# Up-projection weights of the FFN pairs 32 bytes off in longer buffers, and the inverse row sums in the forget weights' buffer

## The chip, the cores and the metric

The kernel runs on one core of one Trainium2 chip. The metric is the time of one execution on the device, in microseconds (us), as the median of several runs. Five engines work side by side and meet through semaphores: TensorE (PE in the profile; its weight loads are listed as PEld), VectorE (DVE), ScalarE (ACT), GpSimd (POOL) and SyncE (SP), whose queue issues most of the DMAs. On-chip memory (SBUF) has 128 partitions; a tile's place is given below as a byte address within each partition, which is the same for all of them.

## The reference

Two layers, each of three sub-layers on x (512 x 1024, float32): an FFN, a mixer with three branches, and a second FFN. Every sub-layer normalises x, shifts and scales it by values computed from c, and adds its gated result to x.

```
def swiglu(h, w_gate, w_up, w_down):
    return (jax.nn.silu(h @ w_gate) * (h @ w_up)) @ w_down

for l in range(2):
    mod = (silu(c) @ w_ada[l] + b_ada[l]).reshape(B, 9, 1024)
    h = modulate(rms_norm(x, norm_gain[l, 0]), mod[:, 0], mod[:, 1])
    x = x + 0.5 * mod[:, 2] * swiglu(h, w_gate[l, 0], w_up[l, 0], w_down[l, 0])   # 1024 -> 2816 -> 1024
    h = modulate(rms_norm(x, norm_gain[l, 1]), mod[:, 3], mod[:, 4])
    x = x + mod[:, 5] * hybrid_mixer(h, ...)
    h = modulate(rms_norm(x, norm_gain[l, 2]), mod[:, 6], mod[:, 7])
    x = x + 0.5 * mod[:, 8] * swiglu(h, w_gate[l, 1], w_up[l, 1], w_down[l, 1])
```

The mixer's branches are a chunked attention with a learned bias (a), a pooling branch (b) and a forgetting attention (c), whose per-head forget gates come from a small projection of h (1024 to 8). Both attentions divide by the row sums of their softmax.

## The kernel before

**Number format.** A product of float32 operands is made of three matmuls of a 32-bit matmul type: each operand is split into a high part (a cast by ScalarE) and a low part (a subtraction by VectorE), and `triple` (lines 117 to 122) issues high x high, high x low and low x high into the same accumulator. In the profile these are lines 119, 120 and 121. The first name behind the arrow is the moving operand, the second the stationary one (the weights, loaded by a PEld instruction of 128 x 128).

**FFN.** The 2816 hidden channels are 22 tiles of 128. They are worked in four parts of 6, 6, 4 and 6 tiles (`PARTS`). The first four or six tiles of the first part are worked one at a time (`plain`): 128 x 128 weights against all 512 tokens. All others are worked two at a time (`gate_up_pair`, `pair`): the 2 x 2 block product of two weight tiles, two halves of the 1024 channels and two halves of the tokens is done in seven block products in place of eight, as in Strassen's scheme. Each of the seven is 4 x 3 matmuls with 256 moving columns, so a pair of gate tiles and a pair of up tiles are 84 matmuls each. The order of the seven is that of the `prod` calls: a11, a12, s1, s2, a22, s4, s3. From the second part on, the up tiles are worked so too (`whole`); that is 8 up pairs in each of the four FFNs, 32 in all.

**Where the pairs' weights lie.** `pair_weights` makes the seven weight operands out of two loaded tiles. For gate tiles (`which` 0), a11, a12, s1 and a22 lie in `ptb` buffers (high and low part in one buffer), s2 and s4 in two `v2` buffers, s3 in two `strip` buffers. For up tiles (`which` 1), six of the seven lie in the three `whi` buffers (high parts) and the three `wlo` buffers (low parts), and s3 lies in one `v2` buffer. The same `whi` and `wlo` buffers hold the split weights of every other product of the program (`wchunk`): plain FFN tiles, the down projection, and all of the mixer. The moving operands of a pair are `hhi` and `hlo` (the split input) and block sums of it in `b` buffers; the high part of the sum for s3 lies in `pta`.

**Addresses.** A tag (the third argument of `st`) names a group of equal buffers; the groups lie one after another in the order of their first use, each buffer rounded up to 32 bytes. In the built program before the change, `hhi`, `hlo`, `b`, `xv`, `whi`, `wlo`, `ssum`, `t1` and `v2` begin at multiples of 128 bytes. Behind them follow small tiles of the normalisation, and `raw`, `pta`, `ptb`, `strip` and `t2` begin 32 bytes past a multiple of 128. Every step within these tiles that a pair uses is a multiple of 512 bytes.

**Order of the work.** A Python-side scheduler (`later`, `poll`) places small jobs between matmuls by a running count of PE work. Each engine then executes its own list in order; so does the SP queue with its DMAs: a DMA that waits for a buffer holds back all DMAs behind it. A DMA stands in the SP list at a place that depends on when its buffer comes free.

**Forget weights and row sums.** `forget` loads the 128 x 64 forget weights into the one `wf` buffer (256 bytes per partition), once in each layer (line 956). In each attention, `send` (line 1084) is called four times, for two heads each: it transposes the inverse row sums into PSUM, ScalarE copies them into the one `flat` buffer (512 bytes per partition on 8 partitions, line 1090), and POOL's queue writes them to memory (line 1092), from where `spread` reads them back to 64 partitions (line 1098).

Of the kernel before, what the change touches and what calls it, by code (L numbers as in the profile page):

```python
# [15 lines left out]
F32 = mybir.dt.float32  # L16
F32R = mybir.dt.float32r
# [5 lines left out]
P = 128  # L23
T = 512
D = 1024
# [6 lines left out]
NT = T // P  # L32
# [8 lines left out]
def encoder_kernel(tc, xT, c, w_ada, b_ada, gains, w_gate, w_up, w_down, w_qkv, w_f, w_ubg,  # L41
# [18 lines left out]
    def nm(s):  # L60
        uid[0] += 1
        return f"{s}_{uid[0]}"

    def st(shape, dt, tag, bufs):
        return sb.tile(shape, dt, tag=tag, bufs=bufs, name=nm(tag))

    def acc(shape=(P, T)):
        return ps.tile(list(shape), F32, tag="acc", bufs=4, name=nm("acc"))

    def mmt(shape=(P, T)):  # L70
        return ps.tile(list(shape), F32, tag="mm", bufs=4, name=nm("mm"))
# [26 lines left out]
    def later(delay, fn, group=None):  # L98
        t = Task(pe[0] + delay, fn, group)
        tasks.append(t)  # L100
        return t
# [77 lines left out]
    @contextlib.contextmanager  # L179
    def after(what):  # L180

        if what in last:
            with tc.issue_after(last[what]):
                yield
        else:
            yield
# [192 lines left out]
    def split_to(hi, lo, src, lo_eng=nc.vector):  # L379
        nc.scalar.copy(hi, src)  # L380
        return lo_eng.tensor_tensor(lo, src, hi.bitcast(F32), op=ALU.subtract).ins  # L381
# [61 lines left out]
    PARTS = (6, 6, 4, 6)  # L443
    UP_FROM = 1
    SPIN = (4, 0, 7, 3)


    class Ffn:
# [78 lines left out]
        def pair_weights(self, n, which=0):  # L527

            shape = [P, 2, 4, P]
            d = []  # L530
            if which:
                d = [(st(shape, F32R, "whi", 3), st(shape, F32R, "wlo", 3)) for _ in range(3)]
                both = st(shape, F32R, "v2", 4)
                e = (both[:, 0], both[:, 1])
            else:
                for _ in range(2):
                    both = st([P, 2] + shape[1:], F32R, "ptb", 2)
                    d.append((both[:, 0], both[:, 1]))
                d.append((st(shape, F32R, "v2", 4), st(shape, F32R, "v2", 4)))
                e = (st([P, 4, P], F32R, "strip", 2), st([P, 4, P], F32R, "strip", 2))  # L540
            r = [st(shape, F32, *(("raw", NRAW) if which else ("b", NB))) for _ in range(2)]
            for i in range(2):
                last["dma"] = nc.sync.dma_start(r[i].rearrange("p a k c -> p (a k) c"),
                                                (w_gate, w_up)[which][self.l, self.s, n + i]).ins
            s3 = st([P, 4, P], F32, "ssum", 1)
            a11, a12, a21, a22 = r[0][:, 0], r[0][:, 1], r[1][:, 0], r[1][:, 1]
            g = nc.vector.tensor_tensor

            def sums():
                split_to(*d[0], r[0])  # L550
                g(s3, a11, a21, op=ALU.subtract)
                g(a21, a21, a22, op=ALU.add)

            def more():
                g(a11, a21, a11, op=ALU.subtract)
                g(a12, a12, a11, op=ALU.subtract)
                split_to(*d[2], r[0])

            steps = [sums, lambda: split_to(*d[1], r[1]), more, lambda: split_to(*e, s3)]
            w = lambda i, j: (d[i][0][:, j], d[i][1][:, j])  # L560
            tiles = {"a11": w(0, 0), "a12": w(0, 1), "s1": w(1, 0), "a22": w(1, 1), "s2": w(2, 0), "s4": w(2, 1), "s3": e}
            return tiles, steps
# [170 lines left out]
        def start(self):  # L733
# [3 lines left out]
            def spin(operands, n):  # L737
                for z in range(n):
                    mm(acc((P, P)), ones, operands[z % len(operands)][:, :P], start=True, stop=True)
# [4 lines left out]
            for half in range(2):  # L744
# [3 lines left out]
                for tile_ in four[2:]:  # L748
                    fold = nc.vector.tensor_tensor(ssum, ssum, tile_, op=ALU.add)
                spin(four, SPIN[half])  # L750
                for t in range(NT):
                    last["sum"] = mm(pv[:, t:t + 1], ssum[:, t * P:(t + 1) * P], ones[:, 0:1], start=False,
                                     stop=half == 1, skip_group_check=True).ins
            spin([ssum], SPIN[2])
            gate["vector"] = fold.ins
# [14 lines left out]
            with after("turn"):  # L770
                spin([dg[:, 3, :]], SPIN[3])
            pgs = [(acc(), acc()), (acc(), acc()), (mmt(), mmt())]
# [232 lines left out]
    def attention(qs, ks, vs, strip, ys, filler, budget, group):  # L1005
# [5 lines left out]
        def logits(h, group_, strips):  # L1011
            p, odd = divmod(h, 2)
            (q, ql), k = qs[p], ks[p]
            s, lg, pr = mmt(), t1(T), t2(T)
            at = 0
            for i in group_:
                n = (i + 1) * P
                for z in (q, ql):
                    mm(s[:, at:at + n], z[:, odd, i * P:(i + 1) * P], k[:, odd, :n], start=z is q, stop=z is ql)
                at += n  # L1020
            at = 0
            for i in group_:
                n = (i + 1) * P
                mx = st([P, 1], F32, "mx", 4)
                nc.vector.tensor_tensor_reduce(out=lg[:, at:at + n], in0=s[:, at:at + n], in1=strips[i], scale=-1.0,
                                               scalar=BIG, op0=ALU.add, op1=ALU.min, accum_out=mx)
                if odd == 0 and i == 0:
                    sums[p] = st([P, 2 * NT], F32, "sm", 2)
                nc.scalar.activation(pr[:, at:at + n], lg[:, at:at + n], AF.Exp, bias=mx, scale=-1.0,
                                     accum_out=sums[p][:, odd * NT + i:odd * NT + i + 1])  # L1030
                pe[0] += 0.5 * (i + 1.5)
                at += n
            if odd and i == NT - 1:
                later(LAG_S, lambda: send(p), group)
            later(LAG_T, lambda: turn(h, group_, pr), group)
# [48 lines left out]
        def send(p):  # L1084
            rs = st([P, 2 * NT], F32, "rs", 1)
            nc.vector.reciprocal(rs, sums[p])
            tp = mmt()
            nc.tensor.transpose(tp[:2 * NT, :P], rs, ident)
            flat = st([2 * NT, P], F32, "flat", 1)
            nc.scalar.copy(flat, tp[:2 * NT, :P])  # L1090
            pe[0] += 0.5
            nc.gpsimd.dma_start(inv_dram[group, p], flat)
            later(LAG_R, lambda: spread(p), group)

        def spread(p):
            for off in range(2):
                r = inv_dram[group, p].rearrange("(h i) q -> h (i q)", h=2)[off:off + 1, :]
                nc.gpsimd.dma_start(rows_of[p][off * HD:(off + 1) * HD, 1, :], r.broadcast_to([HD, T]))
            later(LAG_N, lambda: norm_rows(p), group)
# [293 lines left out]
```

## Time and profile before

| what | value |
|---|---|
| median of 3 runs | 2378.53 us (2377.65 to 2382.12) |
| the profiled execution's own time | 2377.12 us |
| its span, first to last instruction | 2375.4 us |
| TensorE busy, matmuls | 2356.8 us (99%), 14172 |
| VectorE busy | 1781.4 us (75%) |
| ScalarE busy | 1168.7 us (49%) |
| GpSimd busy | 190.6 us (8%) |
| granted TensorE clock | 1.000 of full speed |

The page of the profile gives the busy time of each engine, the span in 40 slices, the chain of work that ended last, and the costliest groups of instructions. A matmul's duration in it is the time from its start to its modelled end, and the next one starts before that; so the pace of a stream of matmuls is read from the difference of their starts in the timeline, in which a row is: start in us, duration in us, engine, line, operation, tiles (out<-in), shapes and count. A remark in square brackets at a row's end is idle time before it; a row without one followed without a gap.

### The profile page before, as it was taken

The page shows a single profiled execution, that of the slowest core. Times are in us where ns is not written, and L with a number is a line of the kernel's source. Part 1 is how long each engine was busy: PE and PEld are TensorE (multiplying, and loading weights), DVE is VectorE, ACT ScalarE, POOL GpSimd, SP SyncE. Part 2 cuts the span into 40 slices and gives each one's busy share as a digit, 9 for nine tenths or more (in the row PEclk, how much of TensorE's full clock was granted, in tenths as well). Part 3 has the DMA queues.
Part 4 walks back from the last instruction along what each step waited for, and adds up shares of the span by engine and source line. Part 5 has one row for each costly group of instructions (what it writes and reads, how often), then busy time and mean ns, then how long its engine had stood idle before and what let it go on. Part 6 is the DMA issues. An engine that isn't in the chain of part 4 may idle for free. (4 is left out here: it accounts for less than half of the span.)

```text
span 2375.4 us, 36727 instructions
## 1 busy us (share of the span) xinstructions
PE 2356.8 (99%) x14172; PEld 2092.4 (88%) x14172; DVE 1781.4 (75%) x3213; ACT 1168.7 (49%) x2048; POOL 190.6 (8%) x309
## 2 busy tenths in 40 slices
PE   8999999999999999999999999999999999999999
PEld 6898998788888898999998999988888888989998
DVE  7888876787678477888678778776866774767784
ACT  5354455676532353544554444556765324544452
POOL 2000002122220000000100000120222101000000
PEclk9999999999999999999999999999999999999999
DMA  7634433333367425344325333423243763223232
GB/s 278 207 104 155 148 125 99 95 98 120 123 211 265 154 68 187 111 137 150 109 87 188 128 104 134 160 89 99 87 136 114 260 233 133 89 98 123 64 116 89
DMA packets 118484, 325.19 MB, mean 137 GB/s; under 512 B 12034, under 2 KB 14338, under 8 KB 118308
## 3 DMA queue, kind: packets, MB, share of 16 engines
q1 hardware_dynamic: 115106, 314.38, 39.5%
q0 software_dynamic: 3200, 8.46, 1.1%
q8 instruction: 111, 1.82, 0.3%
q14 instruction: 65, 0.53, 0.1%
q10 hardware_dynamic: 2, 0.00, 0.0%
HBM read 316.35 MB, written 6.44 MB: 136 GB/s over the span
## 5 line engine op out<-in xcount | busy, mean ns | idle before, releaser
L272 ACT CAST whi<-raw 128x1024 fp32r<-128x1024 f32 (+1 forms) x260 | 270.4, 1044 | 345.5 <-PE acc L120 196.2
L274 DVE TENSOR_TENSOR wlo<-raw,whi 128x1024 fp32r<-128x1024 f32 (+1 forms) x254 | 310.1, 1225 | 155.1 <-ACT whi L272 153.2
L120 PE MATMUL acc<-b,whi 128*128 128x512 f32 (+1 forms) x704 | 261.1, 371 | 2.0 <-DVE b L381 2.0
L119 PE MATMUL acc<-b,whi 128*128 128x512 f32 (+1 forms) x704 | 262.3, 373 | 0.0
L121 PE MATMUL acc<-b,wlo 128*128 128x512 f32 (+1 forms) x704 | 260.4, 370 | 1.2 <-DVE wlo L274 1.2
L121 PE MATMUL mm<-b,wlo 128*128 128x256 f32 (+1 forms) x768 | 244.8, 319 | 0.3 <-DVE wlo L274 0.3
L120 PE MATMUL mm<-b,whi 128*128 128x256 f32 (+1 forms) x768 | 244.5, 318 | 0.0
L119 PE MATMUL mm<-b,whi 128*128 128x256 f32 (+1 forms) x768 | 244.5, 318 | 0.0
L198 DVE CUSTOM_DVE_ANT_0 v<-v,b,badac 128x1024 f32<-128x1024 f32 x144 | 187.2, 1310 | 19.6 <-DMA v<-in_w_ada_dram 19.5
L120 PE MATMUL mm<-hlo,whi 128*128 128x256 f32 (+1 forms) x616 | 199.1, 323 | 0.0
L121 PE MATMUL mm<-hhi,wlo 128*128 128x256 f32 (+1 forms) x616 | 199.0, 323 | 0.0
L119 PE MATMUL mm<-hhi,whi 128*128 128x256 f32 (+1 forms) x616 | 198.7, 323 | 0.0
L120 PE MATMUL acc<-hlo,whi 128*128 128x512 f32 x480 | 188.1, 392 | 1.7 <-DVE hlo L788 1.6
L119 PE MATMUL acc<-hhi,whi 128*128 128x512 f32 x480 | 187.9, 396 | 1.1 <-ACT hhi L785 1.1
L121 PE MATMUL acc<-hhi,wlo 128*128 128x512 f32 x480 | 187.6, 391 | 0.0
L380 ACT CAST whi<-raw 128x1024 fp32r<-128x1024 f32 x96 | 100.8, 1050 | 136.0 <-PE mm L120 68.0
L121 PEld LDWEIGHTS mm<-b,wlo 128*128 128x128 f32 x768 | 146.3, 190 | 11.2 <-DVE wlo L274 1.2
L120 PEld LDWEIGHTS mm<-b,whi 128*128 128x128 f32 x768 | 146.3, 191 | 10.2
L119 PEld LDWEIGHTS mm<-b,whi 128*128 128x128 f32 x768 | 146.3, 191 | 10.1
L120 PEld LDWEIGHTS acc<-b,whi 128*128 128x128 f32 x704 | 132.7, 189 | 25.2 <-DVE b L381 3.8
L121 PEld LDWEIGHTS acc<-b,wlo 128*128 128x128 f32 x704 | 132.6, 188 | 24.2 <-DVE wlo L274 1.7
L119 PEld LDWEIGHTS acc<-b,whi 128*128 128x128 f32 x704 | 132.7, 189 | 21.6
(326 smaller groups left out, 6116.9 us busy)
## 6 DMA issues: line engine op xcount, KB each, us to landing
v<-in_w_ada_dram SPq DMA_DIRECT2D x144, 512.0 KB, 4.8
raw<-in_w_down_dram SPq DMA_DIRECT2D x88, 512.0 KB, 3.9
raw<-in_w_up_dram SPq DMA_DIRECT2D x82, 512.0 KB, 3.6
b<-in_w_gate_dram SPq DMA_DIRECT2D x76, 512.0 KB, 6.0
raw<-in_w_ubg_dram SPq DMA_DIRECT2D x56, 512.0 KB, 4.1
raw<-in_w_qkv_dram SPq DMA_DIRECT2D x42, 512.0 KB, 4.0
raw<-in_w_branch_dram SPq DMA_DIRECT2D x24, 512.0 KB, 3.6
raw<-in_w_out_dram SPq DMA_DIRECT2D x16, 512.0 KB, 3.7
```

Source lines behind the costliest of these rows:

```text
L119: mm(o, lh, rh, start=start, stop=False, skip_group_check=onto)
L120: mm(o, lh, rl, start=False, stop=False, skip_group_check=onto)
L121: mm(o, ll, rh, start=False, stop=stop, skip_group_check=onto)
L198: dot = nc.vector.tensor_tensor_reduce(out=raw, in0=raw, in1=silc[0], scale=1.0, scalar=badac[:, l, j, d:d + 1], op0=ALU.mult, op1=ALU.add ...
L272: nc.scalar.copy(hi, raw)
L274: last["lo"] = lo_eng.tensor_tensor(lo, raw, hi.bitcast(F32), op=ALU.subtract).ins
L380: nc.scalar.copy(hi, src)
```

## The change

Two edits. In `pair_weights`, the six up-pair operands in `whi` and `wlo` are views that begin 8 elements (32 bytes) into a buffer of 1024 + 16 elements, so that the group's buffers are 4160 bytes long in place of 4096. `wchunk` still takes its tiles from the start of the same buffers. In `send`, the tile of the inverse row sums takes its buffer from the group `wf`, which grows from 256 to 512 bytes; the group `flat` is gone.

```
     PARTS = (6, 6, 4, 6)
     UP_FROM = 1
     SPIN = (4, 0, 7, 3)
+    SHIFT = 8
...
             shape = [P, 2, 4, P]
             d = []
             if which:
-                d = [(st(shape, F32R, "whi", 3), st(shape, F32R, "wlo", 3)) for _ in range(3)]
+                d = [tuple(st([P, D + 2 * SHIFT], F32R, t, 3)[:, SHIFT:SHIFT + D].rearrange("p (a k c) -> p a k c", a=2, k=4)
+                           for t in ("whi", "wlo")) for _ in range(3)]
                 both = st(shape, F32R, "v2", 4)
                 e = (both[:, 0], both[:, 1])
...
             nc.vector.reciprocal(rs, sums[p])
             tp = mmt()
             nc.tensor.transpose(tp[:2 * NT, :P], rs, ident)
-            flat = st([2 * NT, P], F32, "flat", 1)
+            flat = st([2 * NT, P], F32, "wf", 1)
             nc.scalar.copy(flat, tp[:2 * NT, :P])
```

What the built program makes of it, as bytes past a multiple of 128:

| tiles | before | after |
|---|---|---|
| `hhi`, `hlo`, `b`, `xv`, `ssum`, `t1`, `v2` | 0 | 0 |
| `whi`, the three buffers, used from their start | 0, 0, 0 | 0, 64, 0 |
| `wlo`, the three buffers, used from their start | 0, 0, 0 | 64, 0, 64 |
| up pairs' six operands in `whi` / `wlo` | 0 / 0 | 32, 96, 32 / 96, 32, 96 |
| `raw`, `pta`, `ptb`, `strip`, `t2` | 32 | 32 |

In numbers of matmuls: 2304 with 256 columns (32 pairs x 72) get weights 32 bytes past a multiple of 64. Without such a shift, weights 64 bytes past a multiple of 128 are met by 2160 matmuls with 512 columns and 400 with 256, and a moving operand there by 448 with 512.

The order of the instructions on PE, DVE, ACT and POOL is the same. On the SP queue one DMA moves: the load of layer 1's forget weights, whose buffer is now also that of the row sums. These are the rows of the SP queue in layer 0 around its place before, at the mixer's first projections (`raw` are the loads of projection weights):

```order
L261 DMA raw_3628<-in_w_down_dram 128x2x512
L261 DMA raw_4008<-in_w_qkv_dram 128x2x512
L261 DMA raw_4086<-in_w_qkv_dram 128x2x512
L956 DMA wf_16368<-in_w_f_dram 128x64
L261 DMA raw_4116<-in_w_qkv_dram 128x2x512
L261 DMA raw_4146<-in_w_qkv_dram 128x2x512
```

In the changed kernel the rows there follow each other without it:

```order
L261 DMA raw_3628<-in_w_down_dram 128x2x512
L261 DMA raw_4008<-in_w_qkv_dram 128x2x512
L261 DMA raw_4086<-in_w_qkv_dram 128x2x512
L261 DMA raw_4116<-in_w_qkv_dram 128x2x512
L261 DMA raw_4146<-in_w_qkv_dram 128x2x512
```

The DMA now stands later in layer 0, behind the last branch load of the forgetting attention's stretch and ahead of the load of the pooling weights (`t`) and of silu(c) (`b`). The SP queue there in the changed kernel:

```order
L261 DMA raw_6999<-in_w_ubg_dram 128x1024
L261 DMA raw_7060<-in_w_branch_dram 128x2x512
L958 DMA wf_16368<-in_w_f_dram 128x64
L1168 DMA t_1300_6850<-in_w_pool_dram 128x4x128
L1287 DMA b_6848<-sil_dram 128x1024
L261 DMA raw_7066<-in_w_ubg_dram 128x1024
```

Before, `t` followed the branch load at once. What the moved DMA waits for there is the release of its buffer by the last row sums of layer 0, that is, by POOL's write of them to memory. The numbers behind the tiles' names only tell buffers apart.

More of the change, by code (lines that the diff above doesn't have):

```diff
@@ L445, in encoder_kernel @@
     SPIN = (4, 0, 7, 3)
+    SHIFT = 8
     class Ffn:
@@ L531, in pair_weights @@
             if which:
-                d = [(st(shape, F32R, "whi", 3), st(shape, F32R, "wlo", 3)) for _ in range(3)]
+                d = [tuple(st([P, D + 2 * SHIFT], F32R, t, 3)[:, SHIFT:SHIFT + D].rearrange("p (a k c) -> p a k c", a=2, k=4)
+                           for t in ("whi", "wlo")) for _ in range(3)]
                 both = st(shape, F32R, "v2", 4)
@@ L1088, in send @@
             nc.tensor.transpose(tp[:2 * NT, :P], rs, ident)
-            flat = st([2 * NT, P], F32, "flat", 1)
+            flat = st([2 * NT, P], F32, "wf", 1)
             nc.scalar.copy(flat, tp[:2 * NT, :P])
```

## The prediction

> **What bounds the kernel now.** I read the page first, then the windows over the stretches in which up pairs run, then the timeline of TensorE there.
>
> ```profile
> span 2375.4 us, 36727 instructions
> PE 2356.8 (99%) x14172; PEld 2092.4 (88%) x14172; DVE 1781.4 (75%) x3213; ACT 1168.7 (49%) x2048; POOL 190.6 (8%) x309
> ```
>
> TensorE is busy 99% of the span. What shortens its stream of matmuls shortens the kernel; what only moves other engines does nothing until TensorE waits. Next, a stretch of three gate pairs and three up pairs in the second FFN of layer 0, and ten us of it:
>
> ```profile
> core 0: us, PE busy (x) PEld busy (x) DVE busy (x) ACT busy (x) POOL busy (x), PEclk, DMA share, GB/s
> 947.68:1007.75 60.07, 60.07 (x506) 60.07 (x504) 48.74 (x86) 32.10 (x58) 0.00 (x0) 1.00 0.32 99
> 977.70:987.70 10.00, 10.00 (x86) 10.00 (x85) 9.90 (x18) 6.62 (x12) 0.00 (x0) 1.00 0.01 2
> ```
>
> TensorE never waits, at the full granted clock (1.00): 504 matmuls (two more are cut by the window's edges) in 60.07 us, 119.2 ns each. VectorE is at 81%, though at 99% in the second row. The pace inside one pair, by the starts of the matmuls:
>
> ```profile
> 947.68 0.28 PE L119 MATMUL acc<-hhi,ptb 128*128 128x256 f32 x1
> ...
> 951.94 0.28 PE L119 MATMUL acc<-b,v 128*128 128x256 f32 x1
> ...
> 953.37 0.28 PE L119 MATMUL acc<-b,ptb 128*128 128x256 f32 x1
> ...
> 954.79 0.28 PE L119 MATMUL acc<-hhi,v 128*128 128x256 f32 x1
> ...
> 956.23 0.28 PE L119 MATMUL acc<-pta,strip 128*128 128x256 f32 x1
> ...
> 957.65 0.28 PE L119 MATMUL mm<-hhi,whi 128*128 128x256 f32 x1
> ...
> 966.16 0.28 PE L121 MATMUL mm<-hhi,wlo 128*128 128x256 f32 x1
> ```
>
> All are the same matmul, 128 x 128 weights and 256 columns. The gate pair's products with weights in `ptb` (36, then 12) take 4.26 + 1.42 = 5.68 us: 118.3 ns each. The two with weights in `v2` take 1.43 and 1.44 us for 12: 119.2 and 120.0. The one in `strip` takes 1.42: 118.3. The up pair, weights in `whi` and `wlo`, takes 8.51 us for 71 steps: 119.9 each. `ptb` and `strip` lie 32 bytes past a multiple of 64, `v2`, `whi` and `wlo` on one. So the place of the weights costs or saves 1.6 ns of a matmul with 256 columns.
>
> **The shifted weights.** 32 up pairs have 72 matmuls each in `whi` and `wlo`, 2304 in all. Their price changes from 119.9 to 118.3 ns: 2304 x 1.6 ns = 3.7 us, or 0.12 us in each pair. The starts are rounded to 0.01 us, which leaves about 0.3 ns on the difference of the two paces and so 0.7 us on the sum. All of it lies on the path, since TensorE has no gap here. The seventh product (s3, weights in `v2`) stays on its multiple of 64.
>
> What no row shows is high and low parts that alternate between 32 and 96 past a multiple of 128, as the shifted ones do: in `ptb` and `strip` both are at 32. Bounds: 0 us if one operand at 96 brings the even pace back, 4.4 us (3.7 + 0.7) if all run like `ptb`. I take 3.7, because the two paces seen so far go with the place past a multiple of 64, and 96 is 32 past one.
>
> A page speaks against this. The Trainium skill (SBUF — State Buffer, section on the DMA port swizzle) gives SBUF lines of 16 bytes, with a price for crossing to a new line; 32 bytes are two whole lines, so by it the shift alters nothing and the sum would be 0. The rows at 951.94 and 953.37 disagree: weights in `v2` and in `ptb`, two products of one pair, take 1.43 and 1.42 us, and the longer runs go at 119.9 and 118.3 ns.
>
> **Engines that write the shifted tiles.** ScalarE casts and VectorE subtracts into them:
>
> ```profile
> L381 DVE TENSOR_TENSOR wlo<-raw,whi 128x1024 fp32r<-128x1024 f32 x96 | 117.2, 1220 | 23.3 <-ACT whi L380 23.2
> L381 DVE TENSOR_TENSOR ptb<-b,ptb 128x1024 fp32r<-128x1024 f32 x70 | 85.6, 1222 | 32.0 <-ACT ptb L380 31.6
> ```
>
> Writing to `ptb`, 32 bytes off, costs VectorE 1222 ns against 1220 on the multiple: 2 ns in 96 instructions, 0.2 us and not on the path. ScalarE's casts precede these and have the same cover as below. A pair that is 0.12 us shorter leaves VectorE less room, so I looked for how early it is:
>
> ```profile
> 967.48 1.22 DVE L381 TENSOR_TENSOR wlo<-raw,whi 128x1024 fp32r<-128x1024 f32 x1
> 977.67 0.28 PE L119 MATMUL mm<-hhi,whi 128*128 128x256 f32 x1
> ```
>
> The last low part for the second up pair of the stretch is ready at 968.70, and that pair begins at 977.67: 9.0 us of cover against 0.12 lost. Without cover VectorE would set the pace at 48.74 of 60.07 us, which is still shorter. I take 0.
>
> **The plain tiles that come to lie 64 bytes on.** Half of the `whi` and `wlo` buffers now begin 64 bytes past a multiple of 128. No row has 128 columns of weights there. The nearest are the forget projection's weights (40 columns, 160 bytes apart, so at 0, 32, 64 and 96 in turn, each used twice), beside two rows of what a matmul with 512 columns can cost:
>
> ```profile
> 652.04 0.39 PE L121 MATMUL acc<-hhi,wlo 128*128 128x512 f32 x1
> ...
> 663.60 0.39 PE L121 MATMUL acc<-hhi,wlo 128*128 128x512 f32 x1
> ```
>
> ```profile
> 372.26 0.40 PE L119 MATMUL acc<-ptb,hhi 128*128 128x512 f32 x1
> ...
> 376.46 0.50 PE L338 MATMUL mm<-ones,strip 128*128 128x1 f32 x4
> ```
>
> ```profile
> 421.50 0.40 PE L963 MATMUL mm<-hhi,ssum 128*40 128x512 f32 x1
> 421.97 0.39 PE L963 MATMUL mm<-hhi,ssum 128*40 128x512 f32 x1
> 422.42 0.40 PE L963 MATMUL mm<-hhi,ssum 128*40 128x512 f32 x1
> 422.89 0.39 PE L119 MATMUL acc<-whi,hhi 128*128 128x512 f32 x1
> ```
>
> All on multiples of 128: 51 steps in 11.56 us, 226.7 ns. Moving operand 32 past (`ptb`): 18 in 4.20 us, 233.3 ns; so here being off is slower, by 6.7. The forget weights, two matmuls each: 0.47 us at 32, 0.45 at 64, 0.47 at 96. So 64 does not run like 32 and 96, and its 225 ns a matmul are nearest to the 226.7 on multiples of 128. I take 0 for the 2160 + 448 matmuls of 512 columns. The bounds: if 64 were like 32 by these rows (235 ns), 2608 x 8.3 = 21.6 us more; if it really gave 225 to the 2160, 3.7 us less, and with the 400 of 256 columns at 1.6 ns 0.6 more of that.
>
> **The moved load of the forget weights.** Before, it was issued as soon as its old contents were read, and blocked nothing:
>
> ```profile
> 377.32 0.34 SPq L956 DMA_DIRECT2D wf<-in_w_f_dram  x1
> 388.59 43.13 SPq L261 DMA_DIRECT2D raw<-in_w_qkv_dram  x9
> ```
>
> The next load came 11 us later, held by its own buffer; taking the DMA away gives 0. At its new place it waits for POOL's last write of the row sums:
>
> ```profile
> 647.21 0.51 POOL L1092 DMA_DIRECT2D inv_dram_c<-flat  x1 [8.65 <-ACT flat L1090]
> 649.56 1.08 POOL L1098 DMA_DIRECT2D b<-inv_dram_c  x2 [1.83 <-PE acc L121]
> ```
>
> ```profile
> 648.55 0.42 SPq L1166 DMA_DIRECT2D t<-in_w_pool_dram  x1
> 660.53 2.07 SPq L261 DMA_DIRECT2D raw<-in_w_ubg_dram  x2
> ```
>
> ```profile
> 652.79 0.62 ACT L380 CAST pta<-t 128x512 fp32r<-128x512 f32 x1 [2.02 <-DMA t<-in_w_pool_dram]
> 656.19 0.62 ACT L380 CAST b<-b 128x512 fp32r<-128x512 f32 x1 [2.78 <-DVE b L1105]
> ```
>
> The read-back at 649.56 follows that write's landing, so the forget load goes out at about 649.6 and the pooling weights at about 650.0, 1.4 us later than before, and silu(c) behind them likewise. Late next is ScalarE's cast of them, at 654.2 and done by 654.8; the instruction behind it began at 656.19 for another reason. The next projection load, at 660.53, is not reached. So 0 on the path, with 1.4 us as the price if it were not covered. The shared buffer adds no other wait that bites: the row sums come only behind the forget projection of their own layer, and layer 1's forget weights are not read before layer 1's mixer.
>
> **Sum.** The profiled execution took 2377.1 us, 1.7 more than its span; less 3.7 is 2373.4. The median of the runs shown is 1.4 above it, and I forecast on that scale: 2378.5 - 3.7 = 2374.8 us.
>
> **The rivals.** (1) The pace does not come with the address alone, or not at 96, and stays at 119.9. For it: gate and up pairs differ in PSUM banks, and `ptb` holds high and low part in one buffer. Against it: `strip` holds them in two and runs at 118.3. Time 2378.5. The 16-byte lines of the Trainium skill's SBUF page would give this result. (2) 64 past a multiple of 128 breaks the even step of the 512-column matmuls as 32 does. The place is every plain FFN tile, the down projection and the mixer; it ends above the old time as soon as a matmul there loses 1.4 ns (3.7 us / 2608), and at half the bound, 10.8 us, it gives 2385.6. For it: the 233.3 ns row. Against it: the forget weights at 64. (3) A wait takes the 0.12 us of each pair back, VectorE being at 99% for ten us. Against it: 9.0 us of cover. Time up to 2378.5. (4) The plain tiles at 64 gain too, by the other bound, 3.7 + 0.6: 2370.5. For it: the one 0.45 us step of the forget weights. Against it: two matmuls of 40 columns, rounded to 0.01 us, say little of 2160.
>
> **How the numbers follow.** Forecast 0.57, (1) 0.17, (2) 0.11, (3) 0.05, (4) 0.10. Above or below 0.2% (4.8 us) is about what a measurement of this kernel can tell from no change; the three runs shown differ by 4.5. The forecast's gain, 3.7, lies under that by 1.1, and with the runs' scatter I give it 0.4 to come out as faster, 0.57 and a little to stay within. Faster: 0.57 x 0.4 + 0.10 x 0.9 = 0.32. Slower: nearly all of (2) and a trace of the others, 0.13. Within: 0.55. The range 2371.0 to 2381.0 holds the forecast, (1) and (3) with the runs' scatter and about half of (4), and leaves (2) out.
>
> **What would show it.** In the changed profile the steps of the up pairs' 72 matmuls should go from 119.9 to a mean of 118.3 ns, and the six-pair stretch from 60.07 to 59.72 us with no idle time on TensorE. The 512-column steps should stay at 226.7. The forget load should be issued near 649.6 and the pooling weights' cast begin near 654.2 with TensorE untouched. A longer 512-column step would make the forecast wrong on the slow side, an unchanged 119.9 in the up pairs would make it no change.

## The result, and the profile after

The changed kernel takes 2392.8 us (median; 2390.6 to 2398.2) where the kernel before, run beside it, takes 2381.4 (2377.7 to 2383.5): a ratio of 1.0052, with a 95% interval of 1.0041 to 1.0062. It is slower by about 12 us, and the forecast was 2374.8. The profiled execution took 2393.4 us.

The comparisons of pace below are read as in the prediction: the difference of the starts of two matmuls, divided by the number of steps between them. First the page of the profile after the change:

```profile
span 2391.6 us, 36728 instructions
PE 2370.8 (99%) x14172; PEld 2090.1 (87%) x14172; DVE 1781.6 (74%) x3213; ACT 1165.1 (49%) x2048; POOL 193.7 (8%) x309
```

The span has grown by 16.2 us and TensorE's busy time by 14.0, with the same 14172 matmuls; VectorE's busy time is what it was. So only 2.2 us of the growth is idle time of TensorE; for the rest, its matmuls follow each other more slowly. The timeline of TensorE after the change, for the products of 512 columns that ran at 226.7 ns before (the prediction's rows from 652.04 to 663.60):

```profile
651.71 0.40 PE L119 MATMUL acc<-hhi,whi 128*128 128x512 f32 x1
...
653.76 0.39 PE L119 MATMUL acc<-hhi,whi 128*128 128x512 f32 x1
...
654.45 0.40 PE L119 MATMUL acc<-hhi,whi 128*128 128x512 f32 x1
...
664.16 0.39 PE L119 MATMUL acc<-hhi,whi 128*128 128x512 f32 x1
```

From 651.71 to 653.76 are nine steps, 227.8 ns each; by the built program's addresses both weight tiles there begin on a multiple of 256 bytes. From 654.45 to 664.16 are 42 steps in 9.71 us, 231.2 ns each; there the high and low parts begin 128 and 64 past a multiple of 256, then 64 and 192. This is the same kind of work as in the prediction's rows, at a pace 4.5 ns slower. Next, the timeline of a gate pair and an up pair in the six-pair stretch:

```profile
951.83 0.28 PE L119 MATMUL acc<-hhi,ptb 128*128 128x256 f32 x1
...
956.14 0.28 PE L119 MATMUL acc<-b,v 128*128 128x256 f32 x1
...
961.83 0.29 PE L119 MATMUL mm<-hhi,whi 128*128 128x256 f32 x1
...
970.25 0.28 PE L121 MATMUL mm<-hhi,wlo 128*128 128x256 f32 x1
```

The up pair's 71 steps take 8.42 us, 118.6 ns in place of 119.9: the shift gains here, with four fifths of the forecast's size. But the gate pair's 36 steps with weights in `ptb` take 4.31 us, 119.7 ns in place of 118.3, though nothing in the diff touches them. The windows view of that stretch (columns as in the prediction):

```profile
951.83:1011.79 59.96, 59.96 (x505) 59.94 (x504) 47.84 (x83) 32.01 (x58) 0.00 (x0) 1.00 0.31 98
```

59.96 us in place of 60.07: 0.11 less, where 0.35 was forecast, again without a gap on TensorE and at the full granted clock.

Over the whole execution, the time from each matmul's start to the next one's, summed by the kind of weights in the two traces (worked out from all starts; what a step has above 400 ns at 512 columns, or above 200 at 256, is counted as waiting):

| steps | count | ns per step, before to after | change, us |
|---|---|---|---|
| weights in `whi`, `wlo`, 512 columns, into `acc` | 3168 | 230.0 to 233.4 | +10.7 |
| weights in `whi`, `wlo`, 512 columns, into `mm` | 1464 | 227.7 to 231.1 | +4.9 |
| `whi`, `wlo` moving, 512 columns | 1008 | 235.9 to 237.0 | +1.1 |
| `v2` and `ptb` moving, 512 columns | 216 | 226.7 to 232.6 (`v2`) | +0.7 |
| weights in `whi`, `wlo`, 256 columns, up pairs among them | 3071 | 120.1 to 118.7 (`mm`) | -4.7 |
| weights in `ptb`, 256 columns | 1968 | 118.2 to 119.6 (`acc`) | +2.8 |
| weights in `v2`, 256 columns | 1224 | 119.7 to 118.5 (`acc`) | -1.1 |
| waiting | | | +2.7 |
| all others | | | -1.2 |
| sum | | | +15.9 |

The 4632 matmuls of 512 columns with weights in `whi` and `wlo` carry +15.6 of the 15.9 us, but not all of it is pace. Near 1530 us TensorE waits 3.2 us for a low part from VectorE, and the seven steps behind that wait take about 427 ns each; the granted clock from 1532 to 1540 is 0.79. The trace before has no such steps. Five of the kernels below whose wide tiles all lie on multiples of 256 bytes have seven or eight of them at this point of the program, so they are no effect of the place. With the steps above 300 ns left out, the mean of the 4632 goes from 227.8 to 230.8 ns, which is +13.8 us. The named rows together, with this +13.8, make +12.6 us, and the ratio of 1.0052 is 12.4 us. The two profiled executions are further apart, by 16.2 us: they also differ in waiting and in that slow stretch, and the one before took 2377.1 us, less than its median of 2381.4.

By the place of the weights after the change (the next table), the 13.8 us are 8.6 from weights at 64 and 192, 3.2 from weights at 128, and 2.0 from weights that stayed at 0 between moved ones.

The table of places under "The change" counts past a multiple of 128. Past a multiple of 256, which turned out to matter, they are, before and after:

| tiles | before | after |
|---|---|---|
| `whi`, three buffers | 0, 0, 0 | 0, 64, 128 |
| `wlo`, three buffers | 0, 0, 0 | 192, 0, 64 |
| `ssum`, `t1`, `v2` | 0 | 128 |
| `raw`, `pta`, `ptb`, `strip`, `t2` | 32 | 160 |

The names from `raw` to `t2` are called the late group below. The moved DMA, in the SP queue and on ScalarE after the change:

```profile
649.96 0.33 SPq L958 DMA_DIRECT2D wf<-in_w_f_dram  x1
650.34 0.43 SPq L1168 DMA_DIRECT2D t<-in_w_pool_dram  x1
```

```profile
655.92 0.62 ACT L380 CAST pta<-t 128x512 fp32r<-128x512 f32 x1 [4.34 <-DMA t<-in_w_pool_dram]
```

The forget load goes out at 649.96 (forecast about 649.6) and the pooling weights' cast begins at 655.92 (forecast 654.2); TensorE is then in the run of 42 steps shown above, without a gap.

### The profile page after: what moved, and what is told of

Same layout as the page of the kernel before. It is cut to its first block, busy times and chain, and to the rows that moved or that the text cites. A ratio compares the mean times of both kernels' runs of the same rounds, so it can differ in the third digit from the quotient of the medians.

```text
span 2391.6 us, 36728 instructions
## 1 busy us (share of the span) xinstructions
PE 2370.8 (99%) x14172; PEld 2090.1 (87%) x14172; DVE 1781.6 (74%) x3213; ACT 1165.1 (49%) x2048; POOL 193.7 (8%) x309
```

## The experiments

Five theories were set against each other. **A**: the longer buffers take plain tiles off multiples of 256 bytes, and that breaks the even step at 512 columns. **B**: the 32-byte shift itself slows plain tiles. **C**: the shared buffer and the moved load cost. **D**: only the unequal places of high and low part count. **E**: 32 past a multiple of 64 is what quickens the up pairs. Unless something else is said, the kernel before is what is edited, and ratios are to it.

### The second edit alone

```diff
-            flat = st([2 * NT, P], F32, "flat", 1)
+            flat = st([2 * NT, P], F32, "wf", 1)
```

> The kernel before with the second edit alone: the inverse row sums in the forget weights' buffer, so the forget load moves in SP's list, and no address of whi, wlo, v2, raw, ptb or strip changes. Theory A (the longer buffers move the plain tiles off multiples of 256 bytes and break the even step of 512-column matmuls): within 0.1% of before, 512-column steps at 226 to 227 ns as before. Theory C (the shared buffer and the moved load cost the time): about 12 us slower.

Measured: 2380.2 us, ratio 1.0000 (0.9991 to 1.0009). The shared buffer and the moved DMA cost nothing that shows beyond 2 us either way, where theory C had about 12. Theory C falls.

### Longer buffers, no shift

```diff
-                d = [(st(shape, F32R, "whi", 3), st(shape, F32R, "wlo", 3)) for _ in range(3)]
+                d = [tuple(st([P, D + 16], F32R, t, 3)[:, 0:0 + D].rearrange("p (a k c) -> p a k c", a=2, k=4)
+                           for t in ("whi", "wlo")) for _ in range(3)]
...
-            flat = st([2 * NT, P], F32, "flat", 1)
+            flat = st([2 * NT, P], F32, "wf", 1)
```

> The changed kernel without the 32 bytes: buffers 4160 bytes long, up pairs' tiles at their start, so every tile of whi and wlo lies 0, 64, 128 and 192, 256, 320 past a multiple of 512. Theory A: the 512-column matmuls are as slow as in the changed kernel, about 16 us against before; up pairs now on multiples of 64 run at 114 to 117 ns instead of 118.6, which gives up to 8 us back, so 4 to 16 us slower than before. Theory B (the 32 bytes themselves slow the plain tiles that use the buffers afterwards): as before.

Measured: 2388.2 us, ratio 1.0032 (1.0021 to 1.0044). The timeline of the same 42 steps of 512 columns:

```profile
654.26 0.39 PE L119 MATMUL acc<-hhi,whi 128*128 128x512 f32 x1
...
663.96 0.39 PE L119 MATMUL acc<-hhi,whi 128*128 128x512 f32 x1
```

9.70 us, 231.0 ns: slow without any shift. With the steps above 300 ns left out, the 4632 wide steps take 13.8 us more than before, the same as in the changed kernel, and `ptb` 2.8 more, again the same. So the length of the buffers makes the loss, not the 32 bytes, and theory B falls. The up pairs, now at 0, 64, 128 and 192, gain too: the 3071 steps of 256 columns in the first table above are 7.3 us shorter than before.

### All three plus three buffers 64 bytes past a multiple of 256

```diff
+        if b == 0:
+            st([P, 16], F32, "pad0", 1)
...
+    st([P, 48], F32, "pad1", 1)
...
-            flat = st([2 * NT, P], F32, "flat", 1)
+            flat = st([2 * NT, P], F32, "wf", 1)
```

> The kernel before with whi and wlo as one block 64 bytes on (a pad of 64 bytes ahead of them, 192 behind; row sums in the forget weights' buffer for room): all six buffers 64 past a multiple of 256, equal for high and low parts, all other tiles where they were modulo 256. If the absolute place counts (theory A): 512-column steps of 230 to 232 ns, 10 to 20 us more from them, and 256-column steps with these weights at 114 to 115 ns instead of 120, 2304 x 5.3 = 12 us less in up pairs and 1 to 2 us less in the split down projection; together -4 to +8 us. If only unequal places of high and low parts break the step (theory D): steps of 226.7 and 120 as before, no change.

Measured: 2389.7 us, ratio 1.0044 (1.0030 to 1.0057). High and low part now lie at equal places, and the buffers have their old length. Its timeline, 60 steps of 512 columns in the same run, and an up pair:

```profile
650.71 0.39 PE L119 MATMUL acc<-hhi,whi 128*128 128x512 f32 x1
...
664.71 0.39 PE L119 MATMUL acc<-hhi,whi 128*128 128x512 f32 x1
```

```profile
963.70 0.28 PE L119 MATMUL mm<-hhi,whi 128*128 128x256 f32 x1
...
971.75 0.28 PE L121 MATMUL mm<-hhi,wlo 128*128 128x256 f32 x1
```

14.00 us for 60 steps is 233.3 ns; 8.05 us for 71 is 113.4 ns. One place, two signs: at 64 a matmul of 512 columns loses 6.6 ns and one of 256 columns gains 6.5. The sums by kind: +26 us for the 4632 wide steps, -18 us for the 3071 narrow ones. Both are larger than expected, and the total, about 10.5 us by the ratio, lies above the expected -4 to +8. Theory D falls, since equal places change both paces.

The moving operands `hhi`, `hlo` and `b` lie on multiples of 256 in every run, so one might think of the distance between the two operands instead of the place. The products for s3 of the gate pairs speak against that: there `pta` moves and `strip` holds the weights, and both belong to the late group. The 245 such steps take 117.7 ns with both at 32 (the kernel before) and 120.0 with both at 0 (a run below), at the same distance.

### The shift with all plain tiles left on multiples of 256

The buffers are 4352 bytes long (17 x 256). The room comes from the shared buffer, from two small modulation tiles that take the place of spent ones, and from a causal mask that GpSimd applies in place, in one instruction, instead of adding a stored one.

```diff
-    modc = cp.tile([P, L, 9, KD], F32, name="modc")
-    apre = cp.tile([P, L, 3, KD], F32, name="apre")
+    modc, apre = badac, gainc
...
-                d = [(st(shape, F32R, "whi", 3), st(shape, F32R, "wlo", 3)) for _ in range(3)]
+                d = [tuple(st([P, D + 64], F32R, t, 3)[:, 8:8 + D].rearrange("p (a k c) -> p a k c", a=2, k=4)
+                           for t in ("whi", "wlo")) for _ in range(3)]
...
-            nc.gpsimd.tensor_tensor(dg, dg, cmask, op=ALU.add)
+            nc.gpsimd.affine_select(dg, dg, pattern=[[-1, P]], base=0, channel_multiplier=1,
+                                    compare_op=ALU.is_ge, fill=NEG)
```

> The 32 bytes without the 64: buffers 4352 bytes long, so that every plain tile stays on a multiple of 256, and the up pairs' views begin 32 bytes in. Room comes from the shared buffer, from writing the modulation and the pre-scales over the tiles of their bias and gain, and from applying the causal mask by a select on GpSimd in place of adding a mask tile. Theory A: 512-column steps back at 226 to 227 ns, up pairs at 118.3 to 118.6, so 3 to 4 us faster than before. Theory B: still about 12 us slower.

Measured: 2375.6 us, ratio 0.9982 (0.9974 to 0.9991). An up pair in its timeline, and 54 steps of 512 columns:

```profile
955.23 0.28 PE L119 MATMUL mm<-hhi,whi 128*128 128x256 f32 x1
...
963.62 0.28 PE L121 MATMUL mm<-hhi,wlo 128*128 128x256 f32 x1
```

```profile
650.50 0.39 PE L119 MATMUL acc<-hhi,whi 128*128 128x512 f32 x1
...
662.74 0.39 PE L119 MATMUL acc<-hhi,whi 128*128 128x512 f32 x1
```

8.39 us is 118.2 ns a step, and 12.24 us is 226.7. This kernel is 0.18%, or 4.3 us, faster, with an interval of 2.1 to 6.2; the steps of 256 columns account for 3.9 of it, and the prediction had 3.7. Theory A stands.

### The same with the views 64, and 128, bytes in

```diff
-                d = [tuple(st([P, D + 64], F32R, t, 3)[:, 8:8 + D].rearrange("p (a k c) -> p a k c", a=2, k=4)
+                d = [tuple(st([P, D + 64], F32R, t, 3)[:, 16:16 + D].rearrange("p (a k c) -> p a k c", a=2, k=4)
```

(and 32 in place of 16 for 128 bytes)

> As the 32 bytes without the 64 (buffers of 4352 bytes, plain tiles on multiples of 256), but the up pairs' views begin 64 bytes in. Theory A (the step of a matmul goes by the place of its weights modulo 256; 64 gave 114.1 ns with 256 columns where the whole block lay there): up pairs at 114.1 ns, 2304 x 5.9 = 13.5 us faster than before, 512-column steps unchanged at 226 to 227. Theory E (the 32 bytes past a multiple of 64 are what quickens): 120 ns, no change.

> The same with the views 128 bytes in. Theory A with a period of 256: neither the even 120 nor 114; weights at 128 in the run with the longer buffers alone stepped at 117 to 118 beside uneven neighbours, so 4 to 7 us faster than before. If the period is 128: even 120 again and no change.

Measured: at 64, 2368.6 us, ratio 0.9950 (0.9938 to 0.9962); at 128, 2378.4 us, 0.9990 (0.9981 to 0.9999). An up pair of the one and of the other:

```profile
953.49 0.28 PE L119 MATMUL mm<-hhi,whi 128*128 128x256 f32 x1
...
961.54 0.28 PE L121 MATMUL mm<-hhi,wlo 128*128 128x256 f32 x1
```

```profile
957.36 0.28 PE L119 MATMUL mm<-hhi,whi 128*128 128x256 f32 x1
...
965.79 0.28 PE L121 MATMUL mm<-hhi,wlo 128*128 128x256 f32 x1
```

113.4 and 118.7 ns a step; the gain at 128, 2.4 us by the ratio, is less than the 4 to 7 expected. Theory E falls: 64, a multiple of 64, quickens the pairs most, about four times what 32 does. And 128 is not like 0 (119.9), so the places do not repeat every 128 bytes. In these kernels neighbouring buffers differ by 256 past a multiple of 512 and run alike, so nothing speaks for a period longer than 256. The kernel at 64 beats both kernels of this case.

### The late group moved alone

`pad` is a small tile ahead of `raw`: 32 bytes (group at 64 past a multiple of 256), 96 bytes (at 128), and, with the shared buffer to make room, 224 bytes (at 0).

```diff
+                    st([P, 8], F32, "pad", 1)
```

> The kernel before with one pad of 32 bytes ahead of raw, pta, ptb, strip and t2, which then begin 64 past a multiple of 256 in place of 32; nothing else is moved. Theory A: the gate pairs' weights in ptb (1968 matmuls) and strip (420) go from 118.2 to about 114.1 ns: 2388 x 4.1 = 9.8 us faster than before. Theory E: they go to 120, 4 us slower.

> The kernel before with 96 bytes ahead of the group, so that raw, pta, ptb, strip and t2 lie 128 bytes past a multiple of 256. Theory A: the ptb products step at about 118.8 ns as the up pairs did with their views 128 bytes in, about 1.2 us more than before: 2381.8 us, ratio 1.0005. Rival (each group of tiles has a pace of its own, and the place hardly counts for ptb): 118.2 ns and 2380.6.

> The kernel before with the shared buffer and the group raw, pta, ptb, strip, t2 on a multiple of 256. Theory A: every weight tile is now on a multiple, so the 1968 products with weights in ptb step at 120.0 ns as those in whi and wlo do, 3.5 us more (118.2 to 120.0), and the products of 512 columns that move ptb get faster, 233 to 227 ns (about 0.6 us less): about 2383.5 us, ratio 1.0012. Rival (gate pairs run faster than up pairs for another reason than the place): steps stay at 118.2 and the time at 2380.6.

Measured: at 64, 2379.1 us, ratio 0.9996 (0.9987 to 1.0005); at 128, 2379.8 us, 1.0002 (0.9992 to 1.0011); at 0, 2383.7 us, 1.0014 (1.0004 to 1.0025). Gate pairs of the three, 36 steps each with weights in `ptb`, in the order 64, 128, 0:

```profile
945.76 0.28 PE L119 MATMUL acc<-hhi,ptb 128*128 128x256 f32 x1
...
950.00 0.28 PE L119 MATMUL acc<-b,v 128*128 128x256 f32 x1
```

```profile
968.42 0.28 PE L119 MATMUL acc<-hhi,ptb 128*128 128x256 f32 x1
...
972.70 0.28 PE L119 MATMUL acc<-b,v 128*128 128x256 f32 x1
```

```profile
968.20 0.28 PE L119 MATMUL acc<-hhi,ptb 128*128 128x256 f32 x1
...
972.52 0.28 PE L119 MATMUL acc<-b,v 128*128 128x256 f32 x1
```

117.8, 118.9 and 120.0 ns. At 0 and 128 the gate pairs run as the up pairs did at 0 and 128, and the ratio at 0 is the forecast's (1.0012 expected): gate pairs are faster in the kernel before because `ptb` lies at 32, and not because of their PSUM banks or of high and low parts in one buffer, which are the same here. At 64 the expectation failed: 117.8 in place of about 114.

### Both groups at 64

The views 64 bytes in, and the 32-byte `pad`.

> The pad of 32 bytes and the up pairs' views 64 bytes in on multiples of 256 together. If the two are independent: 13.5 + 9.8 = 23.3 us faster than before, about 0.990 of its time. If VectorE, 81% busy in these stretches, or the loads come late once a pair is 1.0 us shorter: less, with idle time on TensorE ended by DVE or ACT.

Measured: 2365.2 us, ratio 0.9940 (0.9928 to 0.9951), about 14.3 us less than before by the ratio (15.7 by the medians) where 23.3 were expected. Two gate pairs of this one kernel, the first of a stretch and the second, which follows an up pair:

```profile
941.96 0.28 PE L119 MATMUL acc<-hhi,ptb 128*128 128x256 f32 x1
...
946.20 0.28 PE L119 MATMUL acc<-b,v 128*128 128x256 f32 x1
...
961.50 0.29 PE L119 MATMUL acc<-hhi,ptb 128*128 128x256 f32 x1
...
965.59 0.28 PE L119 MATMUL acc<-b,v 128*128 128x256 f32 x1
```

117.8 and 113.6 ns: equal matmuls at equal places, with two paces. By the starts, this holds for the 32 gate pairs of the later parts without exception. The 36 products in `ptb` at the head of each of the twelve stretches run at about 118 ns throughout; in the 20 gate pairs that follow an up pair, all but the first two run at 113 or 114; and the last 12 products in `ptb` of each pair, which come after a product with weights in `v2`, run at about 118 in all 32. With the late group alone at 64 the same 36 products run at about 118 after an up pair too; there the step that enters them takes 115 ns, here 123 to 124. So at 64 two paces occur, and the one that a run of these matmuls has after its first two steps is kept to its end. That is the larger part of why the gain falls short: by the steps, the products in `ptb` give 4.2 us, where 9.8 were expected of them and those in `strip`. The other part is waiting, which the expectation had allowed for: this trace has 6.9 us more of it than the kernel before, with 4.4 us in two waits for a `wlo` tile from VectorE (1.2 before) and 2.4 us in five waits for ScalarE's copies out of the pairs' PSUM banks (none before). What sets the pace at the entry stays open; no run was aimed at it.

### The changed kernel with the late group back at 32

```diff
-    modc = cp.tile([P, L, 9, KD], F32, name="modc")
-    apre = cp.tile([P, L, 3, KD], F32, name="apre")
+    modc, apre = badac, gainc
...
+                    st([P, 32], F32, "pad", 1)
```

(edits of the changed kernel)

> The changed kernel with 128 bytes ahead of the group that begins with raw, so that raw, pta, ptb, strip and t2 lie 32 bytes past a multiple of 256 as before the change, in place of 160 (room from two small modulation tiles that reuse the place of spent ones). Theory A (the place of the weights past a multiple of 256 sets the step): the products with weights in ptb go back from 119.7 to 118.2 ns, about 2.8 us less than the changed kernel, so about 2390.0 us, ratio to before about 1.004; all else stays as in the changed kernel. Rival (the ptb products were slower for another reason, such as the slower stream around them): their steps stay at 119.7 and the time at 2392.8.

Measured: 2389.7 us, ratio 1.0040 (1.0025 to 1.0054). A gate pair:

```profile
953.73 0.28 PE L119 MATMUL acc<-hhi,ptb 128*128 128x256 f32 x1
...
957.99 0.29 PE L119 MATMUL acc<-b,v 128*128 128x256 f32 x1
```

118.3 ns again (after: 119.7). The sums by kind put `ptb` 0.3 us above the kernel before, in place of 2.8, and the wide `whi` and `wlo` steps still 13.8 above, with the steps over 300 ns left out. The two times alone (1.0040 and 1.0052) overlap in their intervals; the steps show it: about 2.5 us of the loss is the late group's, and the rest stays.

## Why the prediction was wrong

**The shifted weights: right in the price, wrong in the rule behind it.** Forecast -3.7 us; -3.9 by the steps with the plain tiles left in place, and 118.2 ns against the 118.3 forecast. In the changed kernel the alternation of 32 and 96, which no row showed, leaves 118.6, so its bound of 0 did not come. But the forecast took the two paces to go with the place past a multiple of 64, and at 64 itself the pairs run at 113.4. That 96, 160 and 224 past a multiple of 256, where four of the six operands lie, come out near the pace at 32 is luck. The seventh product was taken as unmoved, but its `v2` buffer went from 0 to 128 past a multiple of 256. The rule that the prediction takes from the Trainium skill (SBUF — State Buffer, section on the DMA port swizzle), by which 32 bytes would alter nothing, does not account for this: 32, 64 and 128 bytes, all whole lines of 16, gave 118.2, 113.4 and 118.7 ns against 119.9.

**Engines that write the shifted tiles: right.** VectorE's busy time is 1781.6 us against 1781.4, and the stretch shown has no gap. Waiting grew by 2.7 us in all, but in the three kernels that leave `whi` and `wlo` alone and move the late group it also changed, by -0.2, +1.0 and +2.4 us, so it is not put down to the shift.

**The moved load of the forget weights: right.** Ratio 1.0000 for that edit alone.

**The plain tiles that come to lie 64 bytes on: this is the step that failed.** It took 0 for the matmuls of 512 columns, with +21.6 us as the upper bound; the traces show +13.8 for weights in `whi` and `wlo` and +1.8 for moving operands. Two things were wrong in it. First, the pace at 64 was taken from the forget weights, two matmuls of 40 columns at each place, which gave 225 ns; with 128 columns of weights at 64 the pace is 233.3 ns, close to the 235 that the same rows showed at 32 and 96. Those rows could not price a place at all. The timeline of the kernel before, a little ahead of the rows shown, has the forget weights that lie on multiples of 128:

```profile
419.19 0.40 PE L963 MATMUL mm<-hhi,ssum 128*40 128x512 f32 x1
419.66 0.40 PE L963 MATMUL mm<-hhi,ssum 128*40 128x512 f32 x1
...
421.05 0.39 PE L963 MATMUL mm<-hhi,ssum 128*40 128x512 f32 x1
421.50 0.40 PE L963 MATMUL mm<-hhi,ssum 128*40 128x512 f32 x1
```

Two matmuls at 0 past a multiple of 256 take 0.47 us, as the two at 32 and the two at 96 did; two at 128 past a multiple of 256 take 0.45, as the two that stood for 64 did (they lie at 192 past a multiple of 256). Over both layers the single steps range from 224 to 237 ns, with means of 231.6 at 0, 229.4 at 64, and 232.4 at 32 and 96 past a multiple of 128. The 0.45 us taken for 64 was the shortest of the sixteen pairs of matmuls with the same weights. Against rival (4) the prediction itself had said that two matmuls of 40 columns say little of 2160, and this held for the forecast as well. Secondly, places were counted past a multiple of 128. The third `whi` buffer, at 128 past a multiple of 256, was taken as unmoved; in the changed kernel the steps from one high part to the next there take 232.5 ns, against 228.5 for such steps before. So more matmuls were hit than the 2160, by less each than the bound's 8.3 ns.

**What the prediction did not have:** the late group moved from 32 to 160 past a multiple of 256, which the count by 128 hid. It cost 2.8 us on 1968 products with weights in `ptb`. Weights in `v2`, from 0 to 128, gave back 1.1.

**The rivals.** (2) is what happened, in sign and mechanism, though weights at 128 past a multiple of 256 lost as well. It named a loss of 10.8 us on these matmuls, half its bound, and they lost 15.6 (13.8 + 1.8). It decides from 1.4 ns lost per matmul; 3.0 were lost, by more matmuls than were counted. The prediction's own row of 233.3 ns for a moving operand at 32 spoke for it. (4) has a grain of truth, at 256 columns: the 400 plain matmuls there go from 119.8 to 116.6 ns. (1) did not occur, and (3) not in the stretch shown, which has no gap.

## What to carry to other kernels

A pad or a longer buffer moves every tile behind it, so list the places of all tiles before and after, past a multiple of 256 bytes and not only of 128, and cost every matmul whose weights have moved, wide ones first. A place that is good for 256 columns can be bad for 512: give narrow products a shifted view in a buffer whose length is a multiple of 256, and leave the wide ones on the multiple. Where the only row for a price is a handful of small instructions, it belongs in the bounds and not in the sum.

## What was not expected of the hardware

The step of back-to-back matmuls with 128 x 128 weights of 4 bytes depends on where the weights begin past a multiple of 256 bytes (means over all such steps of a kernel, from the starts, those above 150 ns at 256 columns and above 300 at 512 left out; high and low part at the same place unless noted):

| place | 256 columns, ns | 512 columns, ns |
|---|---|---|
| 0 | 119.9 | 227.8 |
| 32 | 118.2 (up pairs), 118.2 (`ptb`) | not run |
| 64 | 113.4 (up pairs), 117.5 (`ptb` alone at 64), 116.1 (`ptb`, up pairs also at 64) | 233.6 |
| 128 | 118.7 (up pairs), 119.1 (`ptb`) | 232.5 (high to high only, in the changed kernel; at 0 such steps take 228.5) |
| 160 | 119.6 (`ptb`) | not run |

The pace is also kept once entered: at 64, 36 `ptb` products in a row run at about 113.5 or at about 118 ns. So gains of this kind are not independent: by the steps, `ptb` at 64 gives 1.4 us alone and 4.2 beside up pairs at 64. Why the place acts with opposite signs on 256 and 512 columns stays open; no run separates the weight load from the reading of the moving operand.
